# A two-layer hybrid trunk on one NeuronCore: adaptive modulation in units of one row, tile 2's weights tied behind the activation sums, activations split by channel halves

## Chip, core and metric

The kernel runs on one core of a Trainium2 chip. A core has TensorE (PE; matmuls, written to PSUM), VectorE (DVE), ScalarE (ACT), GpSimdE (POOL) and SyncE (SP), which in this kernel issues nearly all DMAs. The metric is the device time of one execution in microseconds, as the median of several runs; smaller is better.

## What is computed

One inference step of a diffusion trunk with two layers, 128 context tokens and 512 latent tokens (640 in all, five row tiles of 128), model width 1024, all in float32. Layer 0 mixes tokens by differential attention with 8 heads, layer 1 by a gated linear recurrence. Each layer ends in a dense SwiGLU feed-forward part of width 2816:

```
m = silu(cond) @ w_ada[i] + b_ada[i]          # six vectors of 1024, for context and for latents
h = rmsnorm(x, g_mix) * (1 + m[1]) + m[0];  x = x + m[2] * mixer(h)
h = rmsnorm(x, g_ffn) * (1 + m[4]) + m[3];  x = x + m[5] * swiglu(h)
swiglu(h) = (silu(gt) * up) @ w_ffn_out,  gt, up = split(h @ w_ffn_in)
```

The six vectors `m[0..5]` are the modulation: shift, scale and gate for the mixer, then for the feed-forward part. There is one set for the context (`c_ctx`) and one for the latents (`c`). `w_ada` has 1024 x 6144 values in each layer.

## The kernel before

**Precision by pairs.** Each float32 operand of a large matmul is split into two parts, `hi` (a ScalarE copy into the type fp32r) and `lo = x - hi` (a VectorE or GpSimdE subtraction). Each product takes three matmuls: hi x hi, hi x lo, lo x hi. Weights go through `load_split` or `split` into the tiles `wh` and `wl`, from raw tiles with the tag `wr` (three buffers). All `wr` loads go through `load`, on SyncE's queue.

**How the order comes about.** The program is written for a planner. It simulates the engines, and puts each engine's instructions into one fixed order by trace order and by when their inputs and buffers are ready in that simulation. On the chip each engine then works through its list and waits where an input is late. Three things tie the order by hand: `pe["strict"]` chains TensorE's matmuls in the order of the program (it is switched off in the feed-forward part, L1580, and on again in its last group); `sp["strict"]` did the same for loads and is off from L918 on; `keep_in_program_order(ins)` puts one instruction behind the one that was traced just ahead of it on its engine.

**Entry of the feed-forward part** (`out_and_ffn`). The attention output is multiplied by `w_o` for row tiles 0 to 4 (psr), scaled by a gate and added to the residual rows `xs[t]` (L1546, L1547). `unit_rows(t)` norms a row tile on ScalarE and GpSimdE. `to_rows(t, eng)` turns it by eight TensorE transposes (`ntp`), multiplies by the scale (L1364, VectorE), adds the shift (L1365, on `eng`) into `Hf`, and splits it into hi and lo. The 640 tokens are two halves of 320 (HTOK): the first half's split is `A1hi`, `A1lo`, the second's goes to `A22` and to a part of `S`. Then `sums` makes the sums and differences of quarters that a seven-product scheme needs (it holds up to three `s4` tiles). `to_rows` calls `sums` for row tiles 2, 3 and 4.

**Feed-forward tiles.** There are 22 tiles of 128 columns. Tiles 0 and 1 are multiplied whole (`whole_weights`, `whole_in`, results psgu): first half for both, then second half, each 48 matmuls. Tiles 2 to 21 use seven products of 12 matmuls instead of eight (`ffn_weights`, `ffn_in`; psgu, psg, psu): their weights are split (L169, L170), and four GpSimdE subtractions (L1436 to L1439) make weight differences, which are split too. `ffn_in` yields three times. The tiles form six groups (4, 4, 4, 3, 3, 4). After each group `rows_out` multiplies the group's result `gT` by `w_ffn_out`: for each half of the 1024 output columns and each of five row tiles, 3 matmuls per tile of the group into psr, then `rtmp = psr * gate` on VectorE (L1313) and the residual add `orow` on GpSimdE (L1314). The gates come from DRAM (`half_gates`, L1306). In the last group both halves run together.

**The modulation** is made in pieces beside other work, as Python generators that a loop advances with `take`. `ada(l, m)` keeps a PSUM tile `psada` and multiplies it up from eight rows of `w_ada` (512 KB each, in `wr` tiles) and a bias. `ada_summed(l, m)` does it on VectorE: for 512 columns at a time, eight rows are multiplied by a scalar and summed into two `acc` tiles (L302, L304), and TensorE only adds up the partitions. `ada_parts` is an older form with three rows at a time (tile `ar`). In layer 0's feed-forward part a chain `fill` of three `ada_summed` and three `ada` makes all of layer 1's vectors but `m[2]`, one piece at each yield of `ffn_in`:

```
for _ in ffn_in(f, ffn_weights(f), group, f - f0):
    take(fill)
```

One piece of `ada` is a row; one piece of `ada_summed` is two rows, each loaded where it is used. Layer 0's `m[5]` is made by `gate5 = ada_parts([(0, 5)])` in heads 1 and 2 of the attention.

**Tag h.** `half_tile(name)` gives a tile of 128 x 512 from seven buffers with the tag `h`. It holds the gates, `rtmp`, the residual rows `xc`, `s4`, `acc` and the rows of `ada_summed`.

Of the kernel before, what the change touches and what calls it, by code (L numbers as in the profile page):

```python
# [21 lines left out]
P = 128  # L22
D = 1024
KT = D // P
NT = 5
# [15 lines left out]
def trunk_kernel(ctx: ExitStack, tc: tile.TileContext, I, O):  # L41
# [116 lines left out]

    def split(src, lo_eng, dims):
# [9 lines left out]
        nc.scalar.activation(out[0], src, AF.Copy)  # L169
        lo_eng.tensor_tensor(out[1], src, out[0], ALU.subtract)  # L170
        return out
# [15 lines left out]

    def ada(l, m, ps=None):
        if ps is None:
            ps = mm_tile([P, 256], "psada")  # L190

        def bias_row():
            r = wp.tile([1, D], F32, name="brow", tag="wr", bufs=3)
            load(out=r, in_=I["b_ada"][l : l + 1, m * D : (m + 1) * D])
            return ones_r, r

        def rows(k):
            return cT[:, k, :], load_raw(I["w_ada"][l, k * P : (k + 1) * P, m * D : (m + 1) * D], [D])

        steps = [lambda k=k: rows(k) for k in range(KT)] + [bias_row]  # L200
        for k, step in enumerate(steps):
            lhs, r = step()
            for j in range(4):
                matmul(
                    ps[32 * j : 32 * j + 32, :],
                    lhs,
                    r[:, 256 * j : 256 * j + 256],
                    start=(k == 0),
                    stop=(k == KT),
                )  # L210
# [77 lines left out]

    def ada_summed(l, m, acc_tile):
        R = cp.tile([P, 256], F32, name="adaR", tag="adaR", bufs=1)  # L290
        wa = I["w_ada"][l].rearrange("(k p) n -> p k n", p=P)
        for h in range(2):
            c0 = m * D + 512 * h
            acc = [acc_tile() for _ in range(2)]
            for k in range(0, KT, 2):
                for i in range(2):
                    w = acc_tile()
                    load(out=w, in_=wa[:, k + i, c0 : c0 + 512])
                    for g in range(2):
                        c = cT[:, k + i, g : g + 1]  # L300
                        if k + i == 0:
                            nc.vector.tensor_scalar(acc[g], w, c, None, ALU.mult)  # L302
                        else:
                            nc.vector.scalar_tensor_tensor(acc[g], w, c, acc[g], ALU.mult, ALU.add)  # L304
                yield
# [255 lines left out]
    def attention(regA, hT, o_tiles, xs0):  # L561
        with ExitStack() as sc:
# [721 lines left out]
    def out_and_ffn(l, oT, w_o, open_rows, gcol, xs, reg, xload):  # L1284
        with ExitStack() as sc:
# [70 lines left out]
            def to_rows(t, eng):  # L1356
                g = 0 if t == 0 else 1
                row = xr.pop(t)
                for hf in range(2):
                    tp = turn_x(row, hf)  # L1360
                    ks = slice(4 * hf, 4 * hf + 4)
# [4 lines left out]
                c0, c1 = t * P, min((t + 1) * P, HTOK)  # L1366
                if c0 < c1:
                    split_rows([v[:, :, c0:c1] for v in A1], Hf[:, :, c0:c1])
                c0, c1 = max(t * P - HTOK, 0), (t + 1) * P - HTOK
                if c0 < c1:  # L1370
                    split_rows([v[:, 3, :, c0:c1] for v in S], Hf[:, 0:4, HTOK + c0 : HTOK + c1])
                    split_rows([v[:, :, c0:c1] for v in A22], Hf[:, 4:8, HTOK + c0 : HTOK + c1])
                    sums(c0, c1)

            def sums(c0, c1):
                n = c1 - c0
# [50 lines left out]

            def ffn_weights(f):
# [4 lines left out]
                h1 = split(b11, nc.vector, [4, P])  # L1433
                h2 = split(x2, nc.vector, [4, 2, P])
                ta, tb = (xr_tile().rearrange("p (s k c) -> p s k c", s=2, k=4) for _ in range(2))
                nc.gpsimd.tensor_tensor(ta[:, 0], b12, b11, ALU.subtract)  # L1436
                nc.gpsimd.tensor_tensor(ta[:, 1], b22, b12, ALU.subtract)
# [113 lines left out]

            def acc_tile():
                return half_tile("acc")

            fill = iter(())
            if l == 0:
                fill = chain(
                    ada_summed(1, 0, acc_tile),
                    ada(1, 5),
                    ada_summed(1, 1, acc_tile),  # L1560
                    ada(1, 3),
                    ada_summed(1, 2, acc_tile),
                    ada(1, 4),
                )
# [8 lines left out]
            for gi, (f0, f1) in enumerate(FF_GROUPS):  # L1573
                nk = f1 - f0
                if gi == 0:
                    first.append(whole_weights(1))
                    to_rows(NT - 2, nc.vector)
                    gus = [whole_in(first[0], 0)]
                    to_rows(NT - 1, nc.vector)
                    pe["strict"] = False  # L1580
                    gus.append(whole_in(first[1], 0))
                    open_group(nk)
                    for f, gu in enumerate(gus):
                        put_gT(group, f, 0, gu)
                    for f in range(WHOLE):
                        put_gT(group, f, 1, whole_in(first[f], 1))
                    put_late_sums()
                else:
                    open_group(nk)
                for f in range(max(f0, WHOLE), f1):  # L1590
                    for _ in ffn_in(f, ffn_weights(f), group, f - f0):
                        take(fill)
# [165 lines left out]
```

## Time and profile before

| | us |
|---|---|
| median of the runs (3) | 1879.17 |
| lowest and highest run | 1875.27, 1880.51 |
| the profiled execution, its own time | 1874.95 |
| span of its instructions | 1873.0 |
| busy in the span: TensorE matmul | 1775.6 |
| VectorE | 1282.9 |
| GpSimdE | 905.8 |
| ScalarE | 805.0 |
| mean granted TensorE clock | 0.981 |

A line of a group reads: line of the kernel, engine, operation, tiles written <- read, shape, count, busy us, mean ns of one, and the idle time of the engine before them with what ended it. A wait reads: who waited <- for whom: total us, times, longest. A line of the timeline reads: start, length, engine, line, operation, tiles, and in brackets the idle time just before and what ended it. A line of the windows reads: from:to, length, then busy us and count of PE, PEld (weight loads), DVE, ACT and POOL, the granted TensorE clock, the share of the DMA engines, GB/s.

### The profile page before, as it was taken

Reading aid. Unit: us, or ns where it says so; the run is one execution under the profiler, and the core shown is the slowest. Engines: PE = TensorE matmul, PEld = TensorE weight load, DVE = VectorE, ACT = ScalarE, POOL = GpSimd, SP = SyncE. Lnnn points to the kernel's source line nnn. Section 1 sums busy time; section 2 is a strip of 40 time slices with the busy share of each in tenths; the row PEclk is TensorE's granted clock in tenths of the full one; section 3 lists DMA queues with packets and bytes.
Section 4 is the critical chain, followed back from the end, with each engine's and each line's share of the span. In section 5 each row is a group of like instructions: output and inputs, shape, how many; then the busy total and the mean of one; then the engine's idle time right before and its main releaser. Section 6 shows DMA issues by size and latency. Waiting matters only on the chain.

```text
span 1873.0 us, 34958 instructions
## 1 busy us (share of the span) xinstructions
PE 1775.6 (95%) x13655; PEld 1611.6 (86%) x13655; DVE 1282.9 (68%) x2099; ACT 805.0 (43%) x1764; POOL 905.8 (48%) x924
## 2 busy tenths in 40 slices
PE   6999999998999999988999999999997999999997
PEld 5798999877988888887789999999877998998996
DVE  4877888757874774785577666666858565556666
ACT  3555666635424242332453333333444433433443
POOL 3324454327273635645337555555536275476562
PEclk9999999998999999999999999999998999999999
DMA  9523121553335444443632221212231233333331
GB/s 309 177 65 108 52 74 40 164 171 106 113 114 159 136 144 126 125 154 113 188 110 80 64 61 55 61 55 63 92 110 57 82 90 96 105 95 101 95 105 68
DMA packets 223621, 200.54 MB, mean 107 GB/s; under 512 B 11045, under 2 KB 177367, under 8 KB 223456
## 3 DMA queue, kind: packets, MB, share of 16 engines
q1 hardware_dynamic: 222650, 197.72, 34.1%
q8 instruction: 107, 1.75, 0.4%
q10 hardware_dynamic: 806, 0.60, 0.1%
q14 instruction: 58, 0.48, 0.1%
HBM read 190.90 MB, written 7.37 MB: 106 GB/s over the span
## 4 chain that ended last, share of the span: by engine, by line
PE 67%; DVE 13%; DMA 6%; POOL 6%; issue 5%; ACT 3%; SPq 0%; POOLq 0%; DVEq 0%; ACTq 0%
PE psr L75 14%; PE psgu L75 12%; PE psf L75 8%; PE psqkv L75 8%; PE psu L75 5%; PE psvg L75 5%; POOL orow L1314 3%; DVE acc L304 2%; PE pso L75 2%; PE psg L75 2%; PE S L75 2%; DVE wl L170 2%; PE pa L75 2%; DMA wr<-w_qkv_attn 2%; PE po L75 1%
## 5 line engine op out<-in xcount | busy, mean ns | idle before, releaser
L182 POOL TENSOR_TENSOR wl<-wr,wh 128x341 fp32r<-128x341 f32 (+2 forms) x234 | 219.8, 970 | 190.3 <-ACT wh L178 189.7
L75 PE MATMUL psr<-wh,gT 128*128 128x512 f32 (+1 forms) x888 | 283.6, 392 | 4.3 <-ACT gT L1425 2.5
L178 ACT ACTIVATE wh<-wr 128x1024 fp32r<-128x1024 f32 (+2 forms) x144 | 141.6, 989 | 170.9 <-PE psgu L75 80.5
L75 PEld LDWEIGHTS psr<-wh,gT 128*128 128x128 f32 x888 | 166.4, 189 | 44.0 <-ACT gT L1425 3.2
L75 PE MATMUL psr<-wl,gT 128*128 128x512 f32 (+1 forms) x444 | 173.2, 390 | 0.0
L182 DVE TENSOR_TENSOR wl<-wr,wh 128x1024 fp32r<-128x1024 f32 (+2 forms) x66 | 79.8, 1213 | 129.1 <-ACT wh L178 127.7
L170 DVE TENSOR_TENSOR wl<-xr,wh 128x1024 fp32r<-128x1024 f32 x80 | 124.3, 1557 | 54.8 <-ACT wh L169 54.5
L1314 POOL TENSOR_TENSOR orow<-orow,rtmp 128x512 f32<-128x512 f32 x100 | 159.0, 1621 | 1.6 <-DVE rtmp L1313 1.6
L1496 POOL TENSOR_TENSOR u<-u,p 128x320 f32<-128x320 f32 x40 | 58.1, 1452 | 182.3 <-ACT u L1495 182.3
L170 DVE TENSOR_TENSOR wl<-wr,wh 128x512 fp32r<-128x512 f32 x80 | 101.2, 1268 | 55.6 <-ACT wh L169 55.3
L169 ACT ACTIVATE wh<-wr 128x512 fp32r<-128x512 f32 x80 | 67.6, 845 | 149.5 <-PE psr L75 79.0
L1436 POOL TENSOR_TENSOR xr<-wr 128x512 f32<-128x512 f32 x40 | 58.6, 1466 | 150.1 <-DMA wr<-w_ffn_in 142.5
L169 ACT ACTIVATE wh<-xr 128x1024 fp32r<-128x1024 f32 x80 | 84.1, 1058 | 97.8 <-PE psr L75 45.1
L75 PE MATMUL psf<-Thi,wh 128*128 128x320 f32 x384 | 123.2, 321 | 1.3 <-DVE gt L1042 1.3
L75 PE MATMUL psf<-Tlo,wh 128*128 128x320 f32 x384 | 118.7, 309 | 0.0
L75 PE MATMUL psf<-Thi,wl 128*128 128x320 f32 x384 | 118.6, 309 | 0.0
L1313 DVE TENSOR_TENSOR rtmp<-psr,gate 128x512 f32<-128x512 f32 x129 | 84.1, 683 | 49.1 <-PE psr L75 28.1
L75 PE MATMUL psgu<-Thi,wh 128*128 128x320 f32 x352 | 109.9, 314 | 1.8 <-ACT u L1488 1.6
L75 PE MATMUL psqkv<-wh,Thi 128*128 128x384 f32 x320 | 109.1, 356 | 1.2 <-ACT Thi L603 1.2
L75 PE MATMUL psgu<-Tlo,wh 128*128 128x320 f32 x352 | 109.5, 311 | 0.0
L75 PE MATMUL psgu<-Thi,wl 128*128 128x320 f32 x352 | 109.5, 311 | 0.0
L75 PE MATMUL psu<-Thi,wl 128*128 128x320 f32 x320 | 100.4, 315 | 9.0 <-DVE wl L170 9.0
(316 smaller groups left out, 5670.3 us busy)
## 6 DMA issues: line engine op xcount, KB each, us to landing
wr<-w_ffn_in SPq DMA_DIRECT2D x176, 256.0 KB
wr<-w_ada SPq DMA_DIRECT2D x40, 512.0 KB
wr<-w_ffn_out SPq DMA_DIRECT2D x40, 512.0 KB
ar<-w_ada SPq DMA_DIRECT2D x32, 512.0 KB
wr<-w_in_rec SPq DMA_DIRECT2D x64, 256.0 KB
gate<-gdram SPq DMA_DIRECT2D x56, 256.0 KB
wr<-w_qkv_attn SPq DMA_DIRECT2D x64, 192.0 KB
acc<-w_ada SPq DMA_DIRECT2D x48, 256.0 KB
```

What stands on the lines that cost most here:

```text
L75: in_order(nc.tensor.matmul(*a, **k))
L169: nc.scalar.activation(out[0], src, AF.Copy)
L170: lo_eng.tensor_tensor(out[1], src, out[0], ALU.subtract)
L178: nc.scalar.activation(hi[:, :n], r, AF.Copy)
L182: ins = lo_eng.tensor_tensor(lo[:, cs], r[:, cs], hi[:, cs], ALU.subtract)
L304: nc.vector.scalar_tensor_tensor(acc[g], w, c, acc[g], ALU.mult, ALU.add)
L1313: nc.vector.tensor_tensor(tmp, ps, gates[0 if t == 0 else 1], ALU.mult)
L1314: eng.tensor_tensor(xs[t][:, cs], xs[t][:, cs], tmp, ALU.add)
L1436: nc.gpsimd.tensor_tensor(ta[:, 0], b12, b11, ALU.subtract)
L1496: nc.gpsimd.tensor_tensor(c, c, d, ALU.add)
```

## The change

- `ada` takes its rows as two tiles of 128 x 512 from tag `h`, not one of 128 x 1024 from `wr`, and fetches row k+1 before row k's four matmuls are traced. Its first piece only loads row 0.
- `ada_summed` yields after each row, not after two, and fetches the next row ahead in the same way. Its first piece only loads.
- `gate5` is gone from the attention; `ada(0, 5, ...)` stands at the head of `fill`.
- `fill` advances at five more places in the first group, and after every product of `rows_out` (100 pieces in all, where there were 60).
- `to_rows` turns both halves first, then for each half of the channels multiplies, adds and splits. It no longer calls `sums`. The adds for the last two row tiles go to GpSimdE, not VectorE.
- `sums` for row tiles 2 to 4 is traced after the first-half products of tiles 0 and 1.
- Tile 1's `lo` splits are kept in program order, which places them behind the residual add of the last row tile. Tile 2's weights are traced right behind `sums`, and its first splits and first subtraction are kept in program order.

```
 def ada(l, m, raw_tile):
     def rows(k):
+        out = []
+        for i in range(2):
+            r = raw_tile()
+            n0 = m * D + 512 * i
+            if k < KT:
+                load(out=r, in_=I["w_ada"][l, k * P : (k + 1) * P, n0 : n0 + 512])
...
+    ahead = rows(0)
+    yield
     ps = mm_tile([P, 256], "psada")
+    for k in range(KT + 1):
+        raw, ahead = ahead, rows(k + 1) if k < KT else None
         for j in range(4):
             matmul(...)
...
 def ada_summed(l, m, half_tile):
+    ahead = raw(0)
+    yield
     for h in range(2):
+        acc = [half_tile("acc") for _ in range(2)]
+        for k in range(KT):
+            n = KT * h + k + 1
+            w, ahead = ahead, raw(n) if n < 2 * KT else None
+            for g in range(2):
...
             yield
...
@@ attention
-            gate5 = ada_parts([(0, 5)])
-                    if h in (1, 2) and t:
-                        take(gate5)
@@ rows_out
                         add_rows(ps, t, half, gates, nc.gpsimd if after is None else nc.vector)
+                        take(fill)
@@ to_rows
-                for hf in range(2):
-                    tp = turn_x(row, hf)
+                tps = [turn_x(row, hf) for hf in range(2)]
+                for ks, tp in zip(halves, tps):
...
+                    if c0 < c1:
+                        split_rows([v[:, ks, c0:c1] for v in A1], Hf[:, ks, c0:c1])
-                    sums(c0, c1)
@@ ffn_weights(f, ordered)
+                h1 = split(b11, nc.vector, [4, P], ordered)
+                h2 = split(x2, nc.vector, [4, 2, P], ordered)
+                t1 = nc.gpsimd.tensor_tensor(ta[:, 0], b12, b11, ALU.subtract)
+                if ordered:
+                    tc.keep_in_program_order(t1)
@@ the fill
+                    ada(0, 5, lambda: half_tile("raw")),
                     ada_summed(1, 0, half_tile),
+                    ada(1, 5, lambda: half_tile("raw")),
...
@@ the first group
-                    first.append(whole_weights(1))
-                    to_rows(NT - 2, nc.vector)
+                    first.append(whole_weights(1, nc.vector, True))
+                    to_rows(NT - 2, nc.gpsimd)
+                    take(fill)
                     gus = [whole_in(first[0], 0)]
-                    to_rows(NT - 1, nc.vector)
+                    take(fill)
+                    to_rows(NT - 1, nc.gpsimd)
                     pe["strict"] = False
                     gus.append(whole_in(first[1], 0))
+                    take(fill)
+                    for t in range(2, NT):
+                        sums(t)
+                    weights = ffn_weights(WHOLE, True)
                     open_group(nk)
...
                     for f in range(WHOLE):
                         put_gT(group, f, 1, whole_in(first[f], 1))
+                        take(fill)
```

More of the change, by code (lines that the diff above doesn't have):

```diff
@@ L157, in load_raw, with split @@
         return r[:, :n]
-    def split(src, lo_eng, dims):
+    def split(src, lo_eng, dims, ordered=False):
         n = int(np.prod(dims))
@@ L168, in split @@
             out.append(v)
-        nc.scalar.activation(out[0], src, AF.Copy)
-        lo_eng.tensor_tensor(out[1], src, out[0], ALU.subtract)
+        ins = [nc.scalar.activation(out[0], src, AF.Copy)]
+        ins.append(lo_eng.tensor_tensor(out[1], src, out[0], ALU.subtract))
+        if ordered:
+            for i in ins:
+                tc.keep_in_program_order(i)
         return out
@@ L185, in load_split, with ada @@
         return hi[:, :n], lo[:, :n]
[L188 to L195, printed above, removed]
-        def rows(k):
[L198 to L202, printed above, removed]
+    def ada(l, m, raw_tile):
+        def rows(k):
+            out = []
[4 more added lines that the diff above has]
+                    load(out=r, in_=I["w_ada"][l, k * P : (k + 1) * P, n0 : n0 + 512])
+                else:
+                    r = r[0:1]
+                    load(out=r, in_=I["b_ada"][l : l + 1, n0 : n0 + 512])
+                out.append(r)
+            return out
+        ahead = rows(0)
+        yield
+        ps = mm_tile([P, 256], "psada")
+        for k in range(KT + 1):
+            raw, ahead = ahead, rows(k + 1) if k < KT else None
             for j in range(4):
@@ L287, in ada_parts, with ada_summed, raw @@
         ada_put(*put)
-    def ada_summed(l, m, acc_tile):
+    def ada_summed(l, m, half_tile):
         R = cp.tile([P, 256], F32, name="adaR", tag="adaR", bufs=1)
         wa = I["w_ada"][l].rearrange("(k p) n -> p k n", p=P)
+        def raw(n):
+            h, k = divmod(n, KT)
+            c0 = m * D + 512 * h
+            w = half_tile("raw")
+            load(out=w, in_=wa[:, k, c0 : c0 + 512])
+            return w
+        ahead = raw(0)
+        yield
         for h in range(2):
             c0 = m * D + 512 * h
[L294 to L304, printed above, removed]
+            acc = [half_tile("acc") for _ in range(2)]
[3 more added lines that the diff above has]
+                for g in range(2):
+                    c = cT[:, k, g : g + 1]
+                    if k == 0:
+                        nc.vector.tensor_scalar(acc[g], w, c, None, ALU.mult)
+                    else:
+                        nc.vector.scalar_tensor_tensor(acc[g], w, c, acc[g], ALU.mult, ALU.add)
                 yield
@@ L1358, in to_rows @@
                 row = xr.pop(t)
-                for hf in range(2):
-                    tp = turn_x(row, hf)
-                    ks = slice(4 * hf, 4 * hf + 4)
+                c0, c1 = t * P, min((t + 1) * P, HTOK)
+                d0, d1 = max(t * P - HTOK, 0), (t + 1) * P - HTOK
+                tps = [turn_x(row, hf) for hf in range(2)]
+                halves = [slice(4 * hf, 4 * hf + 4) for hf in range(2)]
+                for ks, tp in zip(halves, tps):
                     ha = Hf[:, ks, t * P : (t + 1) * P]
@@ L1365, in to_rows, with sums @@
                     eng.tensor_tensor(ha, ha, b, ALU.add)
-                c0, c1 = t * P, min((t + 1) * P, HTOK)
-                if c0 < c1:
-                    split_rows([v[:, :, c0:c1] for v in A1], Hf[:, :, c0:c1])
-                c0, c1 = max(t * P - HTOK, 0), (t + 1) * P - HTOK
-                if c0 < c1:
-                    split_rows([v[:, 3, :, c0:c1] for v in S], Hf[:, 0:4, HTOK + c0 : HTOK + c1])
-                    split_rows([v[:, :, c0:c1] for v in A22], Hf[:, 4:8, HTOK + c0 : HTOK + c1])
-                    sums(c0, c1)
-            def sums(c0, c1):
+                    if c0 < c1:
+                        split_rows([v[:, ks, c0:c1] for v in A1], Hf[:, ks, c0:c1])
+                if d0 < d1:
+                    split_rows([v[:, 3, :, d0:d1] for v in S], Hf[:, 0:4, HTOK + d0 : HTOK + d1])
+                    split_rows([v[:, :, d0:d1] for v in A22], Hf[:, 4:8, HTOK + d0 : HTOK + d1])
+            def sums(t):
+                c0, c1 = max(t * P - HTOK, 0), (t + 1) * P - HTOK
                 n = c1 - c0
@@ L1550, in out_and_ffn @@
                     first = [whole_weights(0, nc.gpsimd, l == 0)]
-            def acc_tile():
-                return half_tile("acc")
             fill = iter(())
@@ L1590, in out_and_ffn @@
                 for f in range(max(f0, WHOLE), f1):
-                    for _ in ffn_in(f, ffn_weights(f), group, f - f0):
+                    for _ in ffn_in(f, weights if f == WHOLE else ffn_weights(f), group, f - f0):
                         take(fill)
```

21 lines of the change are left out of this document (9 added, 12 removed).

## The prediction

> **What bounds the kernel now.** The page comes first: does one engine fill the span?
>
> ```profile
> span 1873.0 us, 34958 instructions
> PE 1775.6 (95%) x13655; PEld 1611.6 (86%) x13655; DVE 1282.9 (68%) x2099; ACT 805.0 (43%) x1764; POOL 905.8 (48%) x924
> ```
>
> TensorE is busy for 95% of the span, so work saved on another engine is worth only the TensorE idle time that it removes. The windows by stage tell where that idle time lies. The first window is layer 0's feed-forward part from the last attention-output matmul on, the second the same stretch of layer 1, where no modulation runs beside it; then come two short stretches of layer 0 after a stop.
>
> ```profile
> 444.64:929.80 485.16, 449.47 (x2781) 399.39 (x2781) 342.03 (x423) 179.03 (x307) 242.64 (x162) 0.96 0.44 135
> 1419.79:1871.00 451.21, 431.24 (x2552) 401.56 (x2552) 287.46 (x347) 182.56 (x315) 246.74 (x177) 0.98 0.30 91
> 646.30:653.40 7.10, 5.00 (x24) 4.94 (x24) 7.10 (x9) 0.72 (x1) 3.01 (x2) 0.76 0.18 56
> 802.80:813.70 10.90, 5.74 (x22) 5.66 (x22) 10.90 (x12) 1.06 (x1) 6.95 (x4) 0.69 0.20 61
> ```
>
> The first two numbers are the length and TensorE's busy time. TensorE is idle for 35.7 us in layer 0 and 20.0 us in layer 1. The granted clock was 0.96 and 0.98. VectorE carries 342 us in layer 0 against 287 us. TensorE's waits in the first window say for what it stands (total us, times, longest):
>
> ```profile
> PE psu L75 <- DVE wl L170: 8.0, 3, 5.2
> PE psada L75 <- DVE acc L304: 5.7, 3, 4.7
> PE psada L75 <- DMA wr<-w_ada: 4.7, 3, 2.5
> PE psgu L75 <- DVE A1lo L1354: 3.6, 1, 3.6
> PE psgu L75 <- ACT A1hi L1353: 3.3, 1, 3.3
> PE psada L75 <- DVE u L1498: 1.6, 1, 1.6
> PE psgu L75 <- ACT u L1488: 1.6, 2, 1.4
> PE psg L75 <- DVE wl L170: 1.3, 2, 0.8
> PE ntp L78 <- ACT xr L484: 1.2, 1, 1.2
> ```
>
> The two A1 rows (6.9 us) are the entry: the first product waits for the activations' split. The six rows that name psu, psada, u and wl make 22.9 us; they lie inside the stage, and the modulation is in each, as its own product or as the VectorE sums that stand ahead of a weight split. One of these stops, on VectorE, on SyncE and on TensorE:
>
> ```profile
> 553.79 5.18 DVE L304 SCALAR_TENSOR_TENSOR acc<-acc,cT 128x512 f32<-128x512 f32 x3
> 558.89 1.75 DVE L170 TENSOR_TENSOR wl<-wr,wh 128x512 fp32r<-128x512 f32 x1
> 560.72 2.61 SPq L70 DMA_DIRECT2D wr<-w_ada  x3
> 564.67 1.08 PE L75 MATMUL psada<-wr,cT 128*32 128x256 f32 x8 [2.49 <-DMA wr<-w_ada]
> SPq L70 <- DVE wl L170: 80.2, 32, 9.5
> SPq L1306 <- POOL orow L1314: 28.4, 9, 7.7
> ```
>
> Three sums keep VectorE until 558.9; only then comes the split that frees a slot of the tag wr. SyncE, which had stood for that slot (longest wait for a split 9.5 us), fetches the modulation row at 560.72, and its product runs at 564.67. So weights and modulation rows share three wr slots and one load queue, and each delays the other.
>
> **Part 1: the entry of the two feed-forward parts.** Layer 1 shows it best; VectorE in order, one GpSimdE row, then TensorE:
>
> ```profile
> 1414.76 1.60 DVE L182 TENSOR_TENSOR wl<-wr,wh 128x1024 fp32r<-128x1024 f32 x1 [0.39 <-ACT wh L178]
> 1417.48 2.18 DVE L182 TENSOR_TENSOR wl<-wr,wh 128x1024 fp32r<-128x1024 f32 x1
> 1422.76 1.55 DVE L170 TENSOR_TENSOR wl<-wr,wh 128x512 fp32r<-128x512 f32 x1
> 1425.91 2.28 DVE L170 TENSOR_TENSOR wl<-wr,wh 128x1024 fp32r<-128x1024 f32 x1
> 1429.06 0.68 DVE L1354 TENSOR_TENSOR A1lo<-Hf,A1hi 128x512 fp32r<-128x512 f32 x1
> 1417.29 1.29 POOL L1436 TENSOR_TENSOR xr<-wr 128x512 f32<-128x512 f32 x1
> 1423.26 0.41 PE L75 MATMUL psgu<-A1hi,wh 128*128 128x320 f32 x1 [3.47 <-ACT A1hi L1353]
> 1429.79 0.64 PE L75 MATMUL psgu<-A1lo,wh 128*128 128x320 f32 x1 [6.12 <-DVE A1lo L1354]
> ```
>
> Four weight splits, 7.6 us of VectorE, stand ahead of the last A1lo: two of tile 1 (L182), two of tile 2 (L170). The change ties tile 1's splits behind the residual add of the last row tile, and tile 2's first steps, on all three engines, behind the sums; GpSimdE's 1.29 us ahead of the activation adds goes too. The split by channel halves lets the product start on the first half. Together that is more than the 3.47 + 6.12 = 9.6 us of idle time. I take 8.5 us off, since about 1 us of copies must come between, and 2 us for the slow clock behind the stop (in the 646.30 row 24 matmuls kept TensorE for 5.0 us, where the pace row below gives 24 x 0.141 = 3.4). Layer 0 has 6.9 us; with tile 2's work gone from GpSimdE and VectorE I take 6 us off and 1.5 us of clock. Bounds: from nothing, if other ready work slips into the place, to 11.6 and 8.5 us.
>
> What is late next is tile 2. Its pinned pieces stand behind the sums, and four GpSimdE subtractions and two more splits follow them. From the first product to tile 2's first there are four groups of 48 matmuls, at 0.141 us 27 us. In that time VectorE has tile 1's splits, the sums and tile 2's own splits; before, it had little room there:
>
> ```profile
> 1425.00:1450.00 25.00, 20.21 (x124) 20.20 (x125) 23.02 (x28) 10.70 (x17) 14.40 (x13) 0.80 0.19 64
> ```
>
> VectorE was busy for 23.0 of 25 us. I charge 2 us in each layer (0 to 6), 4 in all. Moving the adds of the last two row tiles to GpSimdE takes four instructions of 0.68 us off VectorE and is inside these figures.
>
> **Part 2: the modulation's units.** The work is the same, but its pace changes:
>
> ```profile
> L304 DVE SCALAR_TENSOR_TENSOR acc<-acc,cT 128x512 f32<-128x512 f32 x84 | 76.6, 949 | 1.1 <-DMA acc<-w_ada 1.1
> L1313 DVE TENSOR_TENSOR rtmp<-psr,gate 128x512 f32<-128x512 f32 x50 | 32.6, 684 | 22.3 <-PE psr L75 13.5 <-DMA gate<-gdram 4.4 <-POOL orow L1314 4.3
> 586.00:595.00 9.00, 9.00 (x64) 9.00 (x63) 2.37 (x4) 3.21 (x5) 1.60 (x1) 1.00 0.47 167
> 528.08:539.87 11.79, 11.79 (x53) 9.76 (x52) 6.63 (x10) 1.70 (x2) 11.71 (x9) 1.00 0.13 45
> ```
>
> A feed-forward tile has 7 x 12 matmuls at 9.00/64 = 0.141 us: 11.8 us. Three units run beside it. A summed unit had four VectorE steps of 0.949 us, so 11.4 us of sums for 11.8 us of TensorE, and VectorE also owes the tile its splits; hence the queue. Now a unit has two, 5.7 us for a tile, and the rest moves into the output products, where each of 50 row tiles takes a unit: 12 matmuls at 11.79/53 = 0.222 us, 2.7 us, against 1.9 us for the sums and 0.68 for rtmp. The rows leave the wr slots and are fetched a unit ahead. That should take most of the 22.9 us. I take two thirds, 15 us, because no order ties the sums behind the splits, so some stops will stay where sums are ready early. The slow clock goes with the stops: the 802.80 row has 22 matmuls in 5.7 us of busy time, 2.6 us over their pace, the 646.30 row 1.6 us over. About five such stops make 10 us, two thirds of it 7. Part 2: -22 (bounds 0 and -33).
>
> A rule speaks against cutting the row loads. The Trainium skill's page "DMA: Bandwidth & Descriptors", section "Rules for kernel authors", wants at least 1 MiB per DMA. By it two loads of 256 KB are worse than one of 512 KB; if each added its fixed time of about 2 us (an estimate from that page's section on the anatomy of one DMA) to a path that nothing covers, the 32 rows that are cut in two would cost 64 us. Here the load of 560.72 stood 3.9 us from issue to product, and a unit ahead is 2.7 to 3.9 us, so I count it as covered.
>
> **Part 3: the gate of layer 0's feed-forward part**, l 0, m 5, leaves heads 1 and 2 of the attention and becomes the first ten units. What it held there, and one modulation unit inside the feed-forward part:
>
> ```profile
> 122.82 1.50 PE L75 MATMUL psada<-ar,cT 128*32 128x256 f32 x24 [1.08 <-DVE o L775]
> PE psada L75 <- DVE o L775: 2.2, 2, 1.1
> 568.64 0.64 PE L75 MATMUL psada<-wr,cT 128*32 128x256 f32 x8
> ```
>
> Three groups of 1.5 us and two waits, 2.2 us, are 6.7 us taken off. Nine products of 0.64 us are 5.8 us added. Net -1 (bounds -3 and +4: the gate is now read back at the end of tile 3, some 2 us before the first rtmp; the six PSUM buffers hold 6 x 2.7 us of products meanwhile).
>
> **Part 4: the tag h.** Its seven buffers now also hold rows: two sums and two rows, or four halves of rows, beside two gates, leave one for rtmp. The product of a row tile then hands over VectorE, GpSimdE, VectorE. GpSimdE was busy for 11.71 of 11.79 us in the 528.08 row with 9 instructions, 1.3 us each; 0.68 + 1.3 = 2.0 us is under 2.7, so it fits. I charge 2 us (bounds -1 and +50, the slower rival).
>
> **Sum:** -8.5 - 2 - 6 - 1.5 + 4 - 22 - 1 + 2 = -35 us. The profiled execution took 1874.95 us, 2 us over its span; less 35 it is 1840. The median of the runs shown is 1879.17, 4 us above it, so I forecast 1844 us.
>
> **Rivals.** (a) The sums still bunch: two thirds of the inner stops stay. For it speaks the x3 row, which ran although a weight split was waiting; against it the halved steps. Part 2 gives -7 and the sum -20: 1859 us. (b) Tile 2 comes late by the whole pinned chain: 6 us in each layer and its slow clock, 2 more; the entry gives -2 in place of -14 and the sum is -23: 1856 us. (c) The pool runs dry (slower): with one h buffer left, the next half's gates can't be fetched until the last rtmp of this half is given back, and SyncE stands there with the next weights behind it. It stood so nine times already, 7.7 us at worst. If TensorE pays 5 us in each of the ten half-stages, +50 turns the sum to +15: 1894 us. It decides from 3.5 us a half on. Against it: 6 PSUM buffers and the next tiles' products. (d) The planner's new order undoes the gains and nothing is seen: 1879 us.
>
> For the clock, the row first: at 646.30 the granted clock was 0.76 after a stop of about 2 us. The Trainium skill's page "TensorE: Matmul & The Clock Gate", section "What's actually happening", lets the clock fall only after an idle window of about 3.4 us. By that rule the short stops would cost no clock, and the 7 us for the clock in Part 2 would be nearer 5. The row here differs, and I go by it.
>
> **Chances.** Forecast 0.52, with its own range 1829 to 1854; (a) 0.18, (b) 0.11, (c) 0.12, (d) 0.07. No change means within 0.3%, 5.6 us, which is about what the spread of the runs lets one tell. Nearly all of the forecast, (a) and (b) is faster: 0.80; (d) and a little of (a): 0.07; (c) and a little of (d): 0.13. The range takes in the forecast, (a) and (b), with a part of (d): 1828 to 1875.
>
> **What would show it.** Right: no L170 or L182 row on VectorE between the last two A1lo rows; idle before the first psgu under 2 us in each layer; no wait of psada for w_ada or acc over 1 us; no psada in heads 1 and 2; runs of L304 of four at most between splits; a granted clock of 0.98 in layer 0's feed-forward part. Wrong: a wait of psg or psu for wl at tile 2, rtmp waiting for orow or for a gate by more than 10 us in all, or SyncE standing on orow for longer than the 28.4 us shown.

## The result, and the profile after

The changed kernel takes 1904.5 us (median of 4 runs, 1899.7 to 1905.5) beside 1877.2 us for the kernel before on the same chip: a ratio of 1.0141, interval 1.0113 to 1.0168. It is 27 us slower, where 35 us less was forecast.

The page's head shows TensorE busy 14.5 us longer than the 1775.6 us of before, in a span that is 30 us longer:

```profile
span 1903.0 us, 35035 instructions
PE 1790.1 (94%) x13655; PEld 1612.1 (85%) x13655; DVE 1297.3 (68%) x2095; ACT 806.8 (42%) x1770; POOL 912.1 (48%) x932
```

The windows by stage say where. They are cut at the same matmuls in both kernels: last attention-output product, first product of tile 2 (psu), first product of the recurrence (psf), last psf; then the last output product of layer 1's mixer, tile 2 of layer 1, end. The first number behind the range is the length, the second TensorE's busy time; the last three numbers are the granted clock, the DMA share and GB/s. The kernel before:

```profile
443.80:489.10 45.30, 37.25 (x237) 35.89 (x236) 42.51 (x51) 23.78 (x40) 27.11 (x20) 0.89 0.24 76
...
489.10:965.40 476.30, 447.90 (x2733) 393.78 (x2733) 328.92 (x417) 175.38 (x306) 225.76 (x158) 0.97 0.46 141
965.40:1312.60 347.20, 341.79 (x4305) 327.18 (x4304) 234.68 (x429) 121.68 (x312) 182.31 (x204) 1.00 0.22 63
1417.80:1464.60 46.80, 37.21 (x236) 36.17 (x235) 41.98 (x49) 23.49 (x40) 25.06 (x19) 0.89 0.21 67
1464.60:1873.00 408.40, 396.02 (x2330) 366.57 (x2328) 247.46 (x300) 160.88 (x279) 223.67 (x159) 0.99 0.31 95
```

The changed kernel:

```profile
434.30:479.00 44.70, 39.91 (x277) 36.01 (x275) 39.59 (x41) 22.68 (x40) 30.52 (x24) 0.96 0.25 78
479.00:993.10 514.10, 463.30 (x2768) 394.12 (x2765) 344.00 (x424) 177.32 (x307) 222.25 (x158) 0.95 0.43 136
993.10:1344.70 351.60, 343.30 (x4305) 328.67 (x4304) 235.80 (x430) 122.40 (x314) 182.36 (x204) 1.00 0.22 64
1451.50:1491.00 39.50, 34.88 (x236) 33.88 (x235) 35.84 (x40) 18.95 (x34) 29.14 (x22) 1.00 0.21 67
1491.00:1903.00 412.00, 396.24 (x2330) 366.62 (x2328) 256.62 (x308) 164.82 (x287) 225.96 (x161) 0.99 0.30 95
```

Up to tile 2 of layer 0 the change is 10.1 us ahead (479.0 against 489.1), nearly all of it in the attention. Then the second row loses 37.8 us: 22.4 us of TensorE idle time (50.8 against 28.4) and 15.4 us of longer busy time, with the clock at 0.95 in place of 0.97 and 35 more matmul records, 32 of them products of the gate that left the attention. The recurrence loses 4.4 us in the window shown (2.9 us of it in one longer wait of psf for gt, 4.2 against 1.3 us) and 1.6 us behind it, layer 1's entry wins 7.3 us, and the tiles behind it give 3.6 us back: 30.0 us in all.

TensorE's waits in that second window name one culprit (total us, times, longest):

```profile
PE psada L75 <- DVE acc L320: 35.6, 4, 14.0
PE psu L75 <- DVE wl L170: 4.0, 2, 3.1
...
PE psada L75 <- DMA raw<-w_ada: 0.4, 1, 0.4
```

The prediction's inner stops for wl and for modulation rows are indeed smaller (psu for wl 4.0 us, where it was 8.0; psada for a row 0.4, where it was 4.7). In their place TensorE stands 35.6 us, in four stops, for VectorE's modulation sums. The timeline of the first of them, VectorE, then two loads on SyncE, then TensorE (start, length), and last SyncE's waits for a buffer that a sum holds, in the whole second window:

```profile
522.23 2.36 DVE L318 TENSOR_SCALAR acc<-raw,cT 128x512 f32<-128x512 f32 x2
524.51 0.68 DVE L1326 TENSOR_TENSOR rtmp<-psr,gate 128x512 f32<-128x512 f32 x1
525.11 2.87 DVE L320 SCALAR_TENSOR_TENSOR acc<-raw,cT,acc 128x512 f32<-128x512 f32 x2
527.90 0.68 DVE L1326 TENSOR_TENSOR rtmp<-psr,gate 128x512 f32<-128x512 f32 x1
528.50 2.44 DVE L320 SCALAR_TENSOR_TENSOR acc<-raw,cT,acc 128x512 f32<-128x512 f32 x2
...
532.60 3.08 DVE L320 SCALAR_TENSOR_TENSOR acc<-raw,cT,acc 128x512 f32<-128x512 f32 x2
...
536.21 3.79 DVE L320 SCALAR_TENSOR_TENSOR acc<-raw,cT,acc 128x512 f32<-128x512 f32 x4
...
546.48 3.42 DVE L320 SCALAR_TENSOR_TENSOR acc<-raw,cT,acc 128x512 f32<-128x512 f32 x2
...
528.01 0.33 SPq L70 DMA_DIRECT2D raw<-w_ada  x1
...
530.97 0.33 SPq L70 DMA_DIRECT2D raw<-w_ada  x1
...
535.36 0.39 PE L75 MATMUL psr<-wh,gT 128*128 128x512 f32 x1
548.28 0.65 PE L75 MATMUL psada<-acc,pick 128*32 128x128 f32 x8 [12.53 <-DVE acc L320]
SPq L70 <- DVE acc L320: 52.6, 28, 5.1
```

TensorE reached its product of the sums at 535.75, and its order lets nothing pass it. A summed vector is made in two halves of 512 columns, each from eight rows. By then four of the half's eight rows were summed; the other four took until 548.2, where the product starts on the first of the two sums: 3.1 us a row. A row's two sums mostly take 2.4 to 3.4 us, where 2 x 0.949 = 1.9 us was forecast, and the load of a later row often goes out only when a sum has given a buffer back: sums end at 527.98 and 530.94, loads start at 528.01 and 530.97, and SyncE stands 28 times for such a buffer.

### The profile page after: what moved, and what is told of

Read it like the earlier page. It is cut to its first block, busy times and chain, and to the rows that moved or that the text cites. A ratio compares the mean times of both kernels' runs of the same rounds, so it can differ in the third digit from the quotient of the medians.

```text
span 1903.0 us, 35035 instructions
## 1 busy us (share of the span) xinstructions
PE 1790.1 (94%) x13655; PEld 1612.1 (85%) x13655; DVE 1297.3 (68%) x2095; ACT 806.8 (42%) x1770; POOL 912.1 (48%) x932
## 4 chain that ended last, share of the span: by engine, by line
PE 54%; DVE 11%; issue 3%; DMA 2%; ACT 1%; POOL 1%; SPq 0%; POOLq 0%; DVEq 0%; ACTq 0%
PE psr L75 14%; PE psgu L75 13%; PE psf L75 8%; PE psu L75 6%; PE psvg L75 5%; PE psg L75 3%; DVE acc L320 2%; DVE wl L170 2%; PE pa L75 2%; PE psada L75 1%; PE po L75 1%; DVE Q L1170 1%; PE pk L75 1%; DVE rtmp L1326 1%; DMA raw<-w_ada 1%
## 5 line engine op out<-in xcount | busy, mean ns | idle before, releaser
L75 PE MATMUL psr<-wh,gT 128*128 128x512 f32 (+1 forms) x888 | 289.9, 398 | 3.5 <-DVE gT L1440 1.9
L75 PE MATMUL psqkv<-wh,Tlo 128*128 128x384 f32 x320 | 105.7, 344 | 0.5 <-DVE Tlo L620 0.5
```

What stands on the lines that cost most here:

```text
L75: in_order(nc.tensor.matmul(*a, **k))
```

## Experiments

Runs 1 and 2 below are the kernels of experiments 1 and 2. Ratios are to the kernel before, timed on the same chip; the changed kernel's own is 1.0141. Beside the runs the kernel before took 1876.0 to 1882.6 us, so a difference of a few us between two runs is better read from their ratios.

**1. No units beside the output products.** Theory: the 50 steps between output products are what costs. Rival: the units as such, or the entry, wherever they stand.

```
 rows_out:   add_rows(ps, t, half, gates, ...)
-            take(fill)
 ffn_in:     for _ in ffn_in(f, ...):
-                take(fill)
+                take(fill, 2)
```

> The changed kernel, but the modulation takes no unit after an output product; two units at each yield of a feed-forward tile take their place (all 100 units still run, as early as before). Theory 1 (TensorE's fixed list holds the product of the finished sums, psada<-acc, between output products, where VectorE's sums come later than planned): the three stops of 12.5, 7.5 and 14.0 us beside psr go, about 45 us with the slow clock behind them, and some of the old stops for wl and w_ada inside the tiles come back (10 to 25 us): 1870 to 1885 us. Theory 2 (it is the unit-by-unit loading through the seven h buffers, wherever the units stand): psada still waits for acc by more than 20 us in all, and the time stays at 1895 to 1910 us.

1865.9 us, ratio 0.9959 (0.9938 to 0.9980). This edit turns 1.4% slower into 0.4% faster, 38.6 us between the medians and 34 us by the ratios. The second window is 479.2 us long, with 27.9 us idle, as before the change (28.4):

```profile
479.40:958.60 479.20, 451.31 (x2768) 394.21 (x2765) 342.07 (x423) 180.15 (x313) 227.81 (x163) 0.98 0.48 148
```

```profile
PE psu L75 <- DVE wl L170: 8.1, 3, 4.0
PE psada L75 <- DVE acc L320: 5.6, 3, 5.1
```

So the loss belongs to the units that stand beside the output products. The run is no test of the halved pace, though: with two units at each yield VectorE has four sums there again, as before the change, and the stop for wl is back at 8.1 us, where it was 8.0 before.

**2. The product of the sums traced three steps later.**

```
 ada_summed:   parts.append((ones_r, brow))
-              yield
+              for _ in range(4):
+                  yield
               ps = mm_tile([P, P], "psada")
```

> The changed kernel with three more empty yields between the last sum of a half and the product of its partial sums (psada<-acc), so that this product is traced 8 to 12 us of TensorE later; loads, sums and slots are as they were. Theory 1 (position in TensorE's list): psada's wait for acc falls from 35.6 us to under 8 us and the time to 1860 to 1872 us. Theory 2 (VectorE and the h slots can't carry a unit in an output product's time): the wait only moves, to psr waiting for rtmp or to later tiles, and the time stays at 1890 to 1905 us.

1884.9 us, ratio 1.0065 (1.0043 to 1.0086): half of the loss goes. The stops for the sums fall from 35.6 to 3.4 us, but other work of VectorE is now late:

```profile
PE psgu L75 <- ACT u L1505: 8.2, 3, 4.0
PE psg L75 <- DVE rtmp L1327: 7.2, 2, 4.8
PE psada L75 <- DVE acc L320: 3.4, 2, 2.1
```

**3. The gate back in the attention (heads 1 and 2), with everything else as changed; and the same on run 1.**

```
 attention:  gate5 = ada_parts([(0, 5)]);  if h in (1, 2) and t: take(gate5)
 fill:       - ada(0, 5, ...)
```

> The changed kernel with the gate vector of layer 0's feed-forward part made in heads 1 and 2 of the attention again; the other 90 units and all else as changed. In the two traces the attention ended 9.5 us sooner without it. If its move is worth having, this kernel loses those 9.5 us and wins some 6 to 10 back in the feed-forward part (nine products, their switches): 1900 to 1910 us. If the ten units at the head are what pushes the sums into the output products, the stops shrink and it runs at 1870 to 1890 us.

> The kernel of e1_norows with the gate vector made in heads 1 and 2 of the attention, as before; 90 units in the feed-forward part. The attention should be 9.5 to 10 us longer, and the feed-forward part lose its nine products and ten units, 6 to 9 us. If the move is worth having: 1867 to 1872 us. If its ten units only crowd the first group: 1858 to 1864 us.

1898.9 us, ratio 1.0128 (1.0103 to 1.0153), and 1870.7 us, ratio 0.9955 (0.9939 to 0.9972). Each lies within the interval of the run it is derived from. The last attention-output product ends at 445.5 us with the gate there and at 435.1 without, so 10 us leave the attention; the same comes back in the feed-forward part. No gain from the move can be seen.

**4. The entry alone on the kernel before; and run 1 with the old entry.**

```
 to_rows: channel halves;  sums(2..4) behind the first products;
 whole_weights(1, nc.vector, True);  ffn_weights(WHOLE, True)     # kept (or, in the second, undone)
 fill, gate5, ada, ada_summed, rows_out as before                 # (in the second: as in run 1)
```

> The kernel before with the entry part of the change alone: activations split by channel halves, sums behind the first products, tile 1's and tile 2's splits kept in order, adds of the last two row tiles on GpSimdE. The modulation is as it was before. From the two traces the entry of layer 1 won 6.2 us (9.6 to 3.4 us idle) and lost 4.3 at tile 2, the entry of layer 0 won 3.5 us. If the parts add up: 1864 to 1876 us, with the wait of psgu for ACT p at tile 2 of 3 us in layer 1. If the entry's later tile 2 upsets the old modulation units beside it: 1880 to 1890 us.

> The kernel of e1_norows with the entry of the feed-forward parts as it was before (splits by whole row tile, sums inside, no order kept, adds of the last two row tiles on VectorE); units, their loads and the gate's move as in e1_norows. e5_entry, the entry alone on the kernel before, gave 1877.8 against 1876.0 us. If the entry is worth nothing here either, because tile 2 gives back what the first product wins: 1862 to 1869 us. If it is worth the 6 us that the first product of layer 1 wins: 1871 to 1875 us.

1877.8 us, ratio 1.0008 (0.9990 to 1.0027), and 1868.3 us, ratio 0.9947 (0.9928 to 0.9965). The entry is worth nothing either way. The windows of the first, layer 1's entry and the stage behind it, show why: 7.2 us won (39.6 against 46.8), 5.8 us given back (414.2 against 408.4).

```profile
1425.30:1464.90 39.60, 36.20 (x237) 35.28 (x236) 36.06 (x40) 19.03 (x33) 28.80 (x22) 0.96 0.22 67
1464.90:1879.10 414.20, 397.59 (x2330) 368.23 (x2328) 254.99 (x308) 165.06 (x287) 225.77 (x161) 0.99 0.31 95
```

**5. The four matmuls of a modulation row kept together on TensorE**, on run 1 and on run 2.

```
-            for j in range(4):
+            for j in (2, 3, 0, 1):
                 matmul(ps[32 * j : 32 * j + 32, :], ...)
+                if j != 2:
+                    tc.keep_in_program_order(pe["last"])
```

> The kernel of e1_norows, with the four products of a modulation row kept together: the first traced one needs the second half of the row, and the others are kept in order behind it. In the traces a visit of TensorE to psada costs 0.65 us with two products as with four, and the changed kernel makes 57 visits, 31 of them with two products or fewer, where the kernel before makes 29 visits, 3 of them small. e1_norows makes 39, 12 of them small. If the visit is what costs, 6 to 10 visits fewer give 4 to 6 us: 1858 to 1863 us. If the half rows' cost lies in the loads (twice as many DMAs), nothing changes: 1864 to 1868 us; if waiting for both halves stops TensorE: 1870 us and more.

> The kernel of e3_late (units beside the output products, the sums' product traced three units later), with the four products of a row kept together as in e6_four. e3_late has 51 visits, 23 small ones. If the visits are what still separates e3_late from e1_norows: 8 to 10 us less, 1875 to 1878 us. If the rest is psr waiting for rtmp and the gates (7 us for rtmp in its trace) through the seven h buffers: 1882 to 1887 us.

1868.8 us, ratio 0.9947 (0.9929 to 0.9965), and 1892.6 us, ratio 1.0075 (1.0046 to 1.0105): no gain. Counted in the trace, psada's stretches of at most four records fell from 12 to 2 and from 23 to 6. That TensorE changes to small products more often is real, but holding four together wins no time.

**6. Run 1 with the products two steps later.**

> The version without units in the output products, with two more empty steps between the second-last sums of a half and the product that adds them up. That version's trace has 5.6 us of TensorE standing for these sums (longest 5.1) and 2.8 us for a raw row; its units also end early, near 832 of 958 us, so that later steps have room. If what is left of that version's stops is the place of the product in TensorE's order: the 5.6 us and the half clock behind them go, 1865.9 falls to 1858 to 1862 (ratio 0.990 to 0.993). Rival, that the stops only move on to the next late work (wl, rtmp): 1864 to 1868, ratio 0.994 to 0.996.

1868.2 us, ratio 0.9953 (0.9935 to 0.9970). The rival holds: psada still stands 5.7 us for sums and now 4.8 us for rows; stops only change their places.

**7. Sums of 8 columns in place of 512**, on the changed kernel and on run 1. These two kernels leave out the other 504 columns of every row but the first of a half.

```
-  nc.vector.scalar_tensor_tensor(acc[g], w, c, acc[g], ALU.mult, ALU.add)
+  nc.vector.scalar_tensor_tensor(acc[g][:, :8], w[:, :8], c, acc[g][:, :8], ALU.mult, ALU.add)
```

> The changed kernel with each of the sums' steps on VectorE cut to 8 of 512 columns, apart from the first row's of a half (leaves that part of the sums out); every row is still loaded, every unit and product stands where it did. Theory that the length of the sums (1.2 to 1.7 us each, two per row) sets the pace of the rows in the output stage and so the TensorE stops of 35.6 us: these stops fall below 8 us and the time to 1862 to 1872. Rival, that the loads' own pace through the shared buffers does it: the stops stay above 20 us, the time at 1890 or more. If the stops go but the time stays at 1878 to 1888, what is left is TensorE's small products beside the output products.

> The version without units in the output products, its sums cut to 8 columns in the same way (the same part left out). It gives the floor against which the run before is read: its difference to this one is what units beside the output products cost when VectorE's sums take next to nothing. If that is TensorE's switches alone (24 to 30 of 0.65 us against some 10 us of products that stand elsewhere here): 5 to 10 us. If it is nothing: within 4 us, and all of the loss of the changed kernel belongs to the sums. Time of this run itself: 1858 to 1866, since its stops for sums were 5.6 us.

1876.8 us, ratio 0.9997 (0.9981 to 1.0013), and 1855.6 us, ratio 0.9892 (0.9871 to 0.9912). The first lies between its theories: the stops only fall from 35.6 to 25.6 us, though one column in 64 is left. But the sums' busy time falls only from 88.5 to 38.7 us (503 ns each), so the edit takes somewhat more than half of their time, not all of it. The pair still differs by 21.2 us, where 5 to 10 were expected at most. The timeline of the first shows what else there is, VectorE and then GpSimdE:

```profile
533.67 1.45 DVE L320 SCALAR_TENSOR_TENSOR acc<-raw,cT,acc 128x8 f32<-128x8 f32 x2
535.97 0.36 DVE L320 SCALAR_TENSOR_TENSOR acc<-raw,cT,acc 128x8 f32<-128x8 f32 x2 [0.85 <-DMA raw<-w_ada]
...
533.83 1.27 POOL L1327 TENSOR_TENSOR orow<-orow,rtmp 128x512 f32<-128x512 f32 x1 [0.70 <-DVE rtmp L1326]
```

Two sums of 8 columns take 0.36 us, or 1.45 us where GpSimdE adds a row tile meanwhile, and then the end is GpSimdE's: 533.67 + 1.45 = 535.12, 533.83 + 1.27 = 535.10. It is so throughout: of the 84 sums of 8 columns 27 took over 0.3 us, and each of these ends within 0.06 us of the end of a GpSimdE instruction. The Trainium skill's page "SBUF — State Buffer", section "SBUF: two separate sides", says that the two engines share a port pair as an exclusive lock, held for a whole instruction. These rows agree: VectorE's pair does not run slower, it ends with the other engine's add.

**8. The output products' row adds on VectorE; then without a row buffer for the gated product.**

```
-  add_rows(ps, t, half, gates, nc.gpsimd if after is None else nc.vector)
+  add_rows(ps, t, half, gates)                                                    # first
+  nc.vector.tensor_tensor(ps, ps, gates[...], ALU.mult)                           # second, where after is None
+  nc.vector.tensor_tensor(xs[t][:, cs], xs[t][:, cs], ps, ALU.add)
```

> The changed kernel with the row adds of the output products on VectorE in place of GpSimdE. In the trace with sums of 8 columns a pair of them took 0.35 us, or 1.45 us where it ended together with a GpSimdE row add (535.12 and 535.10). Theory that VectorE's sums stand behind GpSimdE's adds: per output product VectorE then has 0.68 (gate) + about 0.7 (add) + 2 x 0.74 (sums without GpSimdE beside) = 2.9 us against 2.7 us of TensorE, so the sums nearly keep pace: the stops of 35.6 us fall below 15, the time to 1880 to 1890 (ratio 1.002 to 1.008). Rival, that the loads' pace through the seven shared buffers does it: stops stay above 25, time 1895 to 1905. Rival, that VectorE is now too full: stops as before or longer, 1904 or more.

> As the run before, and the gated product is written back into the PSUM tile, so that the output products need no row buffer of the seven for it. If the shared buffers set the pace of the raw rows: one to two more rows can be under way, the stops go below 8 us and the time is 8 to 15 us under the run before (1868 to 1880). If they do not: within 4 us of the run before. Against it: TensorE's output tile is held some 0.7 us longer, and a wait of psr or psg for VectorE's adds would show it.

1894.1 us, ratio 1.0076 (1.0047 to 1.0105): 10.4 us less. Then 1870.6 us, ratio 0.9953 (0.9932 to 0.9974): another 23.5 us less, and as good as run 1 with the units where the change put them. In the first the sums' mean falls from 1093 ns (88.5 us of busy time) in the changed kernel to 936 ns, but the stops are hardly less:

```profile
L320 DVE SCALAR_TENSOR_TENSOR acc<-raw,cT,acc 128x512 f32<-128x512 f32 x84 | 75.7, 936 | 1.9 <-DMA raw<-w_ada 1.6
```

```profile
PE psada L75 <- DVE acc L320: 31.3, 4, 12.9
```

In the second the stops for sums are 3.7 us, and the sums start early. Its timeline, SyncE and then VectorE:

```profile
503.38 0.82 SPq L1319 DMA_DIRECT2D gate<-gdram  x2
504.30 0.85 SPq L70 DMA_DIRECT2D raw<-w_ada  x2
...
501.65 1.91 DVE L318 TENSOR_SCALAR acc<-raw,cT 128x512 f32<-128x512 f32 x2
509.31 10.44 DVE L320 SCALAR_TENSOR_TENSOR acc<-raw,cT,acc 128x512 f32<-128x512 f32 x10 [5.75 <-DMA raw<-w_ada]
```

The half's sums start at 501.65, not at 522.23, and ten run in one go, while in the changed kernel's trace SyncE has fetched gates at 502.69 and no further row until 518.25. What it gains is thus tied to rtmp's place in the tag. But at that point nobody is seen waiting for a buffer: the changed kernel fetches the half's first row at 486.12, and VectorE later stands idle for 10.7 us without summing it, since its list has the first sums behind the first rtmp (521.62).

```profile
486.12 0.35 SPq L70 DMA_DIRECT2D raw<-w_ada  x1
512.42 1.23 DVE L185 TENSOR_TENSOR wl<-wr,wh 128x1024 fp32r<-128x1024 f32 x1 [10.73 <-ACT wh L181]
```

So this edit acts at least in part through the order that the planner makes, and not through a wait on the chip. Whether another order with rtmp in the tag would do as well is open; more buffers for the tag, and the row buffer taken away with the adds left on GpSimdE, were not tried.

**9. The raw rows on another DMA queue.** In the changed kernel SyncE issues seven weight loads between 503.56 and 518.25. Rival to the buffers: SyncE's fixed order.

```
-  load(out=w, in_=wa[:, k, c0 : c0 + 512])
+  nc.scalar.dma_start(out=w, in_=wa[:, k, c0 : c0 + 512])      # second run: nc.gpsimd
```

> The changed kernel with the raw rows of the summed vectors fetched through ScalarE's DMA queue, not SyncE's. In the changed kernel's trace the first row that is summed on VectorE is issued at 518.25, behind seven weight loads (503.56 to 518.15) in which SyncE stands 10.0 us for u L1514; where gated products need no row buffer, the first rows are issued at 504.30 and the half's sums start at 501.65, not at 522.23, and TensorE's stops for the sums were 3.7 us. If it is SyncE's fixed order that makes the rows late: the sums start some 15 us earlier, TensorE's stops of 35.6 us fall below 10 and the time to 1868 to 1882. If it is the seven shared buffers: the rows come no earlier, stops stay above 25 us and the time above 1893. Rival of its own: ScalarE stands at the row loads and hi copies come late, waits for wh or p by more than 15 us, time above 1905.

> The same with GpSimdE's DMA queue. SyncE's order theory: stops below 10 us, time 1868 to 1882, as in the run before. Shared buffers: stops above 25 us and above 1893. GpSimdE standing for a buffer would hold its row adds and subtractions: then waits for wl, orow or rtmp grow by more than 15 us.

1906.7 us, ratio 1.0134 (1.0115 to 1.0152), and 1914.9 us, ratio 1.0180 (1.0157 to 1.0203). So SyncE's seven weight loads are not what holds the rows. On ScalarE's queue the stops stay (on GpSimdE's they are 49.5 us), and the first sums start at 522.99, as late as ever:

```profile
PE psada L75 <- DVE acc L320: 33.8, 4, 14.4
```

```profile
522.99 2.35 DVE L318 TENSOR_SCALAR acc<-raw,cT 128x512 f32<-128x512 f32 x2
```

A fixed order as such is not ruled out by this. The half's second row (the expectation takes it for the first) now goes out at 518.43, right behind a copy on ScalarE (518.37) and without a wait of its own, and VectorE's first sums again stand behind its first rtmp. The next row load then waits for a sum to give a buffer back, and holds up ScalarE's own copy by 6.9 us (until 525.75). So the late start goes by the planner's order, and the loads behind it wait for buffers.

**10. Both edits of 8 on run 2.**

> The version with its products three steps later, with the row adds of the output products on VectorE. That version had only 3.4 us of stops for sums, but 8.2 us for u and 7.2 us for the row buffers, both VectorE's work behind sums. If GpSimdE's adds are what makes VectorE late: these 15 us mostly go, the time falls from 1885 to 1872 to 1878 (ratio 0.997 to 1.000 to the kernel before). Rival, that the rest of its loss is TensorE's small products and VectorE's 200 sums as such: within 4 us of 1885.

> As the run before, with the gated product written back into PSUM and no row buffer for it. If units in the output products cost nothing once buffers, GpSimdE's adds and the product's place are right: 1862 to 1870, as good as the version without units there (1865.9). If TensorE's 24 more small products remain as cost: 1872 to 1880.

The first takes 1868.3 us, ratio 0.9942 (0.9921 to 0.9962), 16.6 us less than run 2 and better than expected; the waits for sums are down to 0.6 us. So there are two ways to make the units harmless in the output stage: earlier sums (the second of 8), or a later product and no GpSimdE adds beside the sums. The two together are a miss: 1885.9 us, ratio 1.0040 (1.0027 to 1.0054). There the output products wait for their PSUM tiles, which VectorE now holds through two steps:

```profile
PE psr L75 <- DVE orow L1342: 12.9, 5, 5.3
PE psr L75 <- DVE u L1520: 6.3, 2, 5.9
```

In the second of 8 the same two waits are 4.9 and 5.8 us. Why they are longer here is open.

The versions that beat both kernels (run 1 and its variants in 3 to 6, the second of 8, the first of 10) lie at 0.994 to 0.996, and their intervals overlap.

## Why the prediction was wrong, point by point

**Part 2 failed, and with it the sign.** The step is "the rest moves into the output products, where each of 50 row tiles takes a unit: 12 matmuls at 11.79/53 = 0.222 us, 2.7 us, against 1.9 us for the sums and 0.68 for rtmp". Three things were missing. First, 1.9 us is a mean over all places; beside GpSimdE's row adds a pair of sums took 2.4 to 3.4 us, and with rtmp a row needed 3.1 us and more against 2.7. Second, "fetched a unit ahead" needs a buffer, and once the sums ran, tag h often had none until a sum gave one back (52.6 us of waits on SyncE). Third, it said nothing of the product of the sums, for which TensorE stands in its fixed order: what its eight rows are late comes out there as one stop, three of them 7.5 to 14 us long. It forecast -22 us; the second window got 37.8 us longer. The 7 us of this for the clock went the wrong way too: 0.95 was granted there, where it was 0.97 before and 0.98 in run 1.

"That should take most of the 22.9 us" was the second mistake. The stop for wl did halve in the changed kernel, and it does not appear among the waits of the second of 8, which keeps the units where the change put them. Yet TensorE is idle there for 27.3 of 476.6 us, against 28.4 us before: a stop that went at one place came back at another (psr for u and orow, 5.8 and 4.9 us). That run is 0.5% faster than the kernel before, 9 us, and not 35.

**Part 4 had the right place and a wrong size.** Tag h was charged +2 us, with a bound of +50. Taken away in this order, GpSimdE's adds beside the sums are worth 10.4 us and rtmp's row buffer 23.5 us; by the ratios the two together are 1.9%, as much as run 1 wins (1.8%). They need not add up elsewhere: with the later product of run 2 the first wins 16.6 us and the second loses as much again. The test "0.68 + 1.3 = 2.0 us is under 2.7, so it fits" asked if GpSimdE fits into a product's time, not what its add does to VectorE's next instruction.

**Rival (c), the pool runs dry, has the right sign** and forecast 1894 us. Its mechanism was half right: the buffers ran out, but it was not gates that SyncE could not fetch, with 5 us in each of ten half-stages. It was rows and their sums, with three long stops and a short one. Of the two signals that the prediction named for it, SyncE standing on orow did not grow: its gate loads stood 3.0 us for orow, where it was 28.4 us before. The other was there: VectorE's rtmp waited 15.5 us for gates, over the 10 us named; but TensorE's output products waited only 1.1 us for rtmp.

```profile
DVE rtmp L1326 <- DMA gate<-gdram: 15.5, 5, 6.4
```

**Part 1 was right in kind and too large.** Layer 1's entry wins 7.3 us (10.5 forecast), layer 0's 3.2 us in the run with the entry alone (7.5 forecast) and 0.6 us in the changed kernel, where units stand inside it. The wait for A1hi went, but the last A1lo still stops TensorE for 3.4 us in each layer, where under 2 us was named. The named row is there: a weight split between the last two A1lo.

```profile
1451.65 0.93 DVE L1368 TENSOR_TENSOR A1lo<-Hf,A1hi 128x512 fp32r<-128x512 f32 x1
...
1453.70 0.68 DVE L1563 TENSOR_TENSOR orow<-orow,xc 128x512 f32<-128x512 f32 x1
1454.30 2.06 DVE L185 TENSOR_TENSOR wl<-wr,wh 128x1024 fp32r<-128x1024 f32 x1
1456.28 0.41 DVE L1368 TENSOR_TENSOR A1lo<-Hf,A1hi 128x256 fp32r<-128x256 f32 x1
```

The change ties tile 1's splits behind the residual add (1453.70). That is just where the last A1lo becomes ready (its A1hi ends at 1453.93), so the first split, 2.06 us, goes ahead of it. "Tile 2 comes late", charged +2 us in each layer, is there too: TensorE waits 3.44 us for a ScalarE copy in tile 2 of layer 1 and 1.4 us in layer 0.

```profile
1497.60 0.42 PE L75 MATMUL psgu<-Thi,wh 128*128 128x320 f32 x1 [3.44 <-ACT p L1496]
```

With that the entry's -14 us is a zero in the runs (1.0008; 0.9959 against 0.9947 with the old one).

**Part 3, net -1, was right**, in part by luck: both pairs agree within their intervals, but both terms were larger than forecast (10 us out of the attention, not 6.7, and about as much back, not 5.8), and the two errors cancel.

**The load rule did no harm, as forecast**: psada waited 0.4 us for rows of 256 KB in the second window, and VectorE's sums 12.4 us. What a row of 512 KB would have done in their place was not tried. The 64 us that the prediction sets against this go by a figure for the DMA path of another engine than SyncE, and no run here shows such a price.

## What to carry to other kernels

Before work is spread beside another stage, time it by rows of that stage, with the engines that will run beside it, and count the buffers that a prefetch needs at that point: "a unit ahead" is worth nothing in a pool that is full. Where TensorE works through a fixed list, look for the instruction that closes a chain of small steps: delays that no single step shows came out there as one stop of 14 us. And when the wait disappears at one place, look at the other waits of the same engine before the gain is counted.

## What was not expected of the hardware

VectorE's two-input sums take as long as GpSimdE's add that runs beside them: 1.45 us for two sums of 8 columns, 0.36 us without it. Its multiplication of a PSUM tile by a gate does not show this: rtmp took 0.68 or 0.69 us in every row of that stretch.

A group of 4 records of small products on TensorE takes as long as one of 8: 0.62 and 0.64 us in the changed kernel. Longer groups do take longer: 12 records 1.06 us (751.20), 24 records 1.50 us (589.35). The prediction's 0.64 us for a unit of 8 is thus no price that halves with the unit.

```profile
484.38 0.62 PE L75 MATMUL psada<-raw,cT 128*32 128x256 f32 x4
...
494.58 0.64 PE L75 MATMUL psada<-raw,cT 128*32 128x256 f32 x8
```
